# A hybrid decoder layer on one core: a new order of all operations, with more room between TensorE's bursts of small matmuls

## The chip, the core and the metric

The kernel runs on one core of one Trainium2 chip. The core has five engines with their own instruction streams: TensorE (PE, with its weight loads listed apart as PEld), VectorE (DVE), ScalarE (ACT), GpSimd (POOL) and SyncE (SP), which here issues most of the DMA transfers. The metric is the time of one execution on the device in microseconds (us).

## The reference

A decoder sub-layer for 2048 tokens of width 1024, in float32. One input projection gives queries, keys, values and gates of two head groups; the groups run side by side and one output projection joins them:

```python
h = rms_norm(x, norm_w)
proj = jnp.einsum('bsd,de->bse', h, w_in)            # 1024 -> 2816 columns
rq, rk, rv, rg, sq, sk, sv, sg = jnp.split(proj, offsets, axis=-1)
ro = retention(rotary(rq), rotary(rk), rv)           # 4 heads, chunks of 128, a state carried along
ro = group_norm(ro) * ret_norm_w * jax.nn.silu(rg)
so = sliding_window_attention(sq, sk, sv, ...)       # 8 heads, 2 key heads, window 128, sinks, bias
so = so * jax.nn.silu(sg)
x = x + jnp.einsum('bse,ed->bsd', jnp.concatenate([ro, so], -1), w_out)
```

## The kernel before

The four wide products (the input projection in three column groups of 512, 384 and 512 columns, in the program's order, and the output projection) are done by blocks with seven products in place of eight: sums and differences of the blocks of x and of w are formed on VectorE, the seven products run on TensorE, and VectorE and ScalarE add the results together. Each operand is split into a high and a low part (`hi` on ScalarE, `lo` on VectorE), and each product is three passes: high by high, high by low, low by high. In the profile these are the matmuls `acc<-w,x`, with 512, 384 or, at the very end, 128 columns. They run from the first microseconds to the last.

Between runs of `acc` matmuls stand bursts of small ones:

- `m<-ident,kn`: one transpose of normalised keys (16 in all);
- `m<-ks,qT`: the logits of a pair of chunks (8 bursts, 64 matmuls in the program, 128 on the engine, since these take two passes);
- `m<-pT,vn`: weights by values (8 bursts, 72 in the program, 144 on the engine);
- `m<-state,qkT`, `m<-qkT`, `m<-v,qk`, `m<-v,sT`: one step of the retention for a pair of chunks (up to 64 in the program, 128 on the engine). The last step has only the first and the last of the four. Where the fourth part adds to banks that the first part wrote, `outputs` holds its first matmul until the last one of `cross` is through, by an instruction of GpSimd that waits for the one and releases the other (`relay`, `behind`).

Each operation is recorded by `op` with its engine, its reads and writes, and a `go` that issues it. Nothing is issued while it is recorded. `emit` then walks through the table `ORDER` of operation numbers and calls each `go`; where an operation makes a new tile, the next entry of the table `PLACES` says in which numbered buffer it lies, and where it could run on two engines, the table `CHOICE` says on which. `Order.put` ties all instructions into that one order, so each engine gets its instructions in the order of the table. The costs and due times that stand beside the operations aren't read when the kernel is built: they belong to the search that made the tables. Since every instruction is issued from `emit` by way of one helper, nearly all rows of the profile have the same line, L498, and the tiles' names tell them apart.

An entry of `PLACES` decides which earlier tile has to be done with before the new one can be written, and so which waits there are.

Of the kernel before, what the change touches and what calls it, by code (L numbers as in the profile page):

```python
# [124 lines left out]
class Program:  # L125
# [46 lines left out]
    0, 1, 2, 3, 11, 378, 15, 383, 18, 388, 21, 393, 13, 30, 12, 24, 27, 112, 381, 379, 398, 399, 400, 386, 401, 14,  # L172
    380, 402, 403, 404, 405, 406, 407, 382, 408, 409, 4, 16, 17, 384, 410, 387, 385, 411, 412, 33, 389, 390, 115, 413,
    414, 415, 416, 22, 19, 417, 418, 419, 420, 421, 422, 23, 391, 423, 424, 425, 20, 426, 427, 428, 429, 430, 394,
    395, 130, 396, 397, 431, 392, 432, 433, 133, 28, 29, 25, 26, 113, 114, 434, 435, 438, 31, 32, 34, 35, 36, 439,
    116, 436, 440, 118, 121, 117, 119, 120, 131, 38, 132, 40, 42, 122, 64, 41, 43, 123, 75, 437, 442, 136, 443, 441,
    444, 445, 449, 65, 127, 128, 450, 52, 54, 124, 125, 126, 129, 142, 143, 144, 134, 135, 149, 451, 452, 457, 458,
    459, 72, 460, 464, 465, 37, 466, 467, 472, 473, 39, 468, 148, 108, 150, 151, 153, 53, 461, 462, 58, 446, 447, 448,
    158, 44, 463, 45, 139, 140, 141, 474, 475, 55, 476, 137, 138, 477, 478, 46, 213, 145, 469, 159, 60, 479, 480, 481,
    482, 483, 484, 485, 59, 487, 488, 470, 56, 170, 169, 171, 110, 172, 177, 47, 489, 10, 48, 490, 161, 492, 152, 493,  # L180
    160, 491, 494, 109, 173, 162, 164, 155, 214, 495, 500, 501, 299, 305, 179, 146, 57, 191, 180, 147, 486, 502, 503,
    508, 453, 509, 510, 511, 163, 167, 111, 61, 496, 497, 165, 168, 49, 62, 215, 471, 203, 217, 515, 516, 303, 202,
    63, 307, 5, 50, 70, 301, 181, 517, 51, 192, 518, 523, 224, 219, 68, 69, 182, 189, 204, 183, 524, 178, 337, 525,
    526, 527, 528, 529, 530, 531, 311, 533, 534, 535, 536, 185, 190, 300, 504, 538, 507, 205, 209, 206, 225, 71, 309,
    302, 193, 304, 194, 200, 81, 207, 499, 306, 201, 211, 498, 456, 212, 216, 220, 222, 308, 310, 312, 176, 93, 223,
    226, 230, 227, 229, 539, 187, 540, 541, 232, 196, 512, 543, 544, 90, 545, 546, 548, 549, 241, 550, 551, 553, 554,
    555, 233, 234, 84, 556, 558, 559, 333, 228, 239, 240, 542, 331, 9, 235, 236, 560, 561, 563, 197, 184, 313, 237,
    66, 67, 218, 335, 532, 315, 238, 195, 198, 85, 186, 339, 564, 281, 565, 566, 567, 341, 552, 505, 506, 568, 569,
    570, 314, 571, 573, 257, 547, 359, 574, 575, 576, 242, 578, 579, 243, 244, 247, 87, 73, 74, 562, 580, 157, 208,
    581, 321, 86, 78, 245, 246, 94, 248, 557, 332, 334, 249, 250, 513, 537, 336, 338, 340, 454, 95, 258, 343, 357,  # L190
    319, 91, 92, 519, 355, 583, 584, 585, 586, 588, 263, 283, 282, 589, 590, 284, 591, 593, 594, 595, 596, 598, 79,
    80, 599, 600, 601, 251, 252, 349, 317, 253, 345, 264, 7, 210, 347, 603, 604, 605, 577, 514, 520, 521, 254, 606,
    612, 613, 342, 88, 89, 351, 265, 266, 860, 255, 256, 154, 614, 615, 597, 316, 261, 318, 947, 82, 174, 320, 156,
    522, 322, 76, 262, 325, 259, 1412, 344, 346, 348, 350, 572, 616, 617, 582, 621, 622, 623, 624, 352, 361, 175, 6,
    323, 260, 630, 631, 632, 607, 77, 83, 267, 633, 639, 634, 640, 269, 851, 327, 353, 1027, 1028, 938, 625, 641, 270,
    642, 647, 268, 648, 275, 279, 643, 455, 99, 649, 650, 654, 655, 656, 1416, 839, 324, 326, 328, 354, 356, 651, 608,
    609, 657, 661, 658, 329, 277, 231, 358, 635, 102, 1405, 626, 627, 636, 662, 663, 664, 276, 944, 273, 360, 669,
    670, 671, 672, 678, 679, 680, 280, 665, 271, 587, 652, 272, 592, 330, 646, 1417, 673, 681, 687, 688, 188, 278,
    618, 644, 645, 689, 690, 274, 696, 848, 697, 698, 96, 659, 362, 199, 363, 364, 845, 971, 365, 366, 699, 705, 1406,
    367, 368, 941, 369, 370, 371, 372, 660, 706, 707, 1418, 857, 105, 708, 682, 712, 713, 714, 715, 1431, 666, 667,  # L200
    221, 683, 691, 373, 720, 721, 289, 290, 374, 375, 1410, 674, 675, 684, 293, 294, 100, 101, 610, 611, 291, 285,
    292, 376, 377, 602, 700, 722, 723, 728, 939, 729, 950, 940, 97, 98, 637, 676, 619, 620, 653, 106, 107, 692, 694,
    103, 104, 668, 166, 849, 850, 935, 295, 685, 8, 296, 730, 854, 962, 731, 735, 736, 297, 874, 858, 638, 709, 287,
    842, 677, 873, 1473, 298, 737, 738, 286, 744, 745, 739, 740, 742, 695, 743, 840, 859, 686, 746, 747, 701, 288,
    753, 754, 703, 755, 756, 762, 763, 628, 629, 841, 748, 749, 741, 751, 752, 1419, 724, 727, 750, 710, 725, 807,
    757, 1432, 1413, 758, 764, 732, 880, 760, 808, 809, 936, 810, 811, 716, 717, 956, 765, 766, 733, 761, 1414, 951,
    965, 812, 767, 813, 814, 815, 816, 719, 771, 1423, 772, 773, 774, 942, 780, 781, 782, 879, 693, 959, 817, 818,
    819, 820, 702, 711, 718, 775, 776, 778, 726, 861, 734, 821, 822, 1424, 1474, 783, 789, 1434, 759, 768, 1464, 1411,
    1465, 779, 1422, 1427, 790, 791, 843, 937, 1433, 1428, 945, 974, 792, 798, 799, 800, 801, 844, 943, 769, 852,
    1436, 853, 846, 1092, 1437, 1093, 784, 785, 787, 847, 1094, 1095, 866, 1097, 952, 966, 1408, 855, 1098, 1099,  # L210
    1100, 1096, 793, 794, 796, 953, 968, 957, 770, 946, 1404, 1435, 1415, 802, 1102, 856, 1467, 1468, 948, 865, 777,
    1103, 862, 1104, 1105, 788, 949, 885, 1101, 1108, 1109, 1110, 1429, 960, 958, 1440, 1472, 967, 1475, 786, 795,
    1420, 1438, 1111, 1114, 1115, 954, 955, 1425, 1466, 803, 1407, 804, 1116, 704, 864, 875, 876, 1409, 969, 970, 823,
    824, 1469, 963, 964, 1112, 1117, 1458, 1119, 1118, 1120, 1121, 1122, 1124, 1106, 1107, 881, 882, 1477, 1426, 1125,
    1762, 1508, 1430, 1439, 825, 826, 975, 827, 983, 1126, 1127, 961, 972, 1470, 973, 1123, 1441, 1450, 1451, 1421,
    797, 863, 1442, 1443, 1446, 1447, 1130, 1131, 868, 1132, 1133, 1452, 1136, 1137, 1138, 1113, 828, 829, 830, 831,
    832, 833, 1478, 834, 835, 1139, 1140, 836, 837, 867, 980, 977, 1444, 1445, 986, 1141, 1142, 1143, 1144, 1146,
    1147, 1148, 1448, 805, 1454, 886, 1145, 1456, 1149, 1152, 1153, 1154, 838, 1155, 1158, 1159, 1517, 1160, 997,
    1678, 1161, 1471, 1520, 976, 1633, 1516, 869, 870, 981, 887, 888, 978, 1510, 1511, 1449, 989, 1548, 1134, 982,
    1509, 1521, 979, 1156, 1479, 994, 1162, 1157, 1163, 1164, 902, 871, 883, 1549, 872, 1135, 1518, 1512, 1513, 1165,  # L220
    1009, 1166, 1168, 1169, 891, 1455, 1602, 1476, 1170, 1171, 889, 905, 1167, 1174, 1175, 892, 984, 877, 1176, 1177,
    985, 1150, 1151, 1180, 890, 878, 884, 1181, 1182, 1183, 1172, 1173, 1550, 1453, 1457, 911, 1592, 1522, 920, 998,
    999, 1002, 1178, 1557, 1179, 806, 1605, 1606, 1480, 990, 917, 991, 1481, 987, 988, 1459, 1128, 1129, 1185, 895,
    1460, 1184, 1462, 1463, 899, 1593, 995, 996, 1502, 893, 1594, 894, 896, 1186, 1187, 1188, 1189, 1515, 1021, 1005,
    1482, 1483, 1190, 1191, 1192, 1193, 1006, 1519, 1015, 1487, 914, 992, 993, 1195, 1196, 1018, 1493, 1642, 1553,
    1485, 1484, 1197, 1198, 1595, 1488, 1554, 1559, 1012, 1489, 1038, 1003, 1004, 1200, 1201, 1202, 1203, 1199, 1491,
    1205, 1206, 1207, 1000, 1029, 1024, 1208, 1210, 1211, 1212, 1204, 1001, 1551, 1495, 897, 1213, 1215, 1216, 1214,
    1032, 1486, 1494, 1490, 1498, 1041, 1007, 1019, 898, 1492, 1524, 1514, 1497, 1562, 1563, 1686, 1217, 1218, 1496,
    1220, 1221, 1222, 1223, 1597, 1598, 1013, 1014, 1225, 1226, 1227, 1644, 1555, 1219, 1008, 1030, 918, 919, 1601,
# [179 lines left out]
CHOICE = {381: "A", 379: "V", 36: "V", 38: "V", 37: "V", 39: "A", 866: "A", 865: "A", 864: "A", 863: "A", 2189: "A", 2187: "A", 2186: "A", 2188: "A", 2914: "A", 2912: "A", 2915: "A", 2913: "A"}  # L409
# [1461 lines left out]
```

## Time and profile before

| | |
|---|---|
| time, median of 3 runs | 659.26 us (658.93 to 661.24) |
| time of the profiled execution | 658.81 us |
| its span, first to last instruction | 657.04 us |
| PE busy | 652.3 us, 99% of the span |
| DVE busy | 577.4 us, 88% |
| ACT busy | 464.9 us, 71% |
| POOL busy | 41.6 us, 6% |
| granted TensorE clock | 1.00 (2.4 GHz) |
| moved by DMA | 162.94 MB, mean 248 GB/s |

The profiled execution's own time is 1.77 us over its span, and 0.45 us under the median. Times of matmuls in the rows are to be read with care: one that is in flight while the next one starts counts as busy for its whole way through the array, so the mean duration of a matmul is longer than the distance from one start to the next. What a run of matmuls costs is read from the starts of two pieces of the chain, divided by the count.

### The profile page before, as it was taken

Reading aid. Unit: us, or ns where it says so; the run is one execution under the profiler, and the core shown is the slowest. Engines: PE = TensorE matmul, PEld = TensorE weight load, DVE = VectorE, ACT = ScalarE, POOL = GpSimd, SP = SyncE. Lnnn points to the kernel's source line nnn. Section 1 sums busy time; section 2 is a strip of 40 time slices with the busy share of each in tenths; the row PEclk is TensorE's granted clock in tenths of the full one; section 3 lists DMA queues with packets and bytes.
Section 4 is the critical chain, followed back from the end, with each engine's and each line's share of the span. In section 5 each row is a group of like instructions: output and inputs, shape, how many; then the busy total and the mean of one; then the engine's idle time right before and its main releaser. Section 6 shows DMA issues by size and latency. Waiting matters only on the chain.

```text
span 657.0 us, 16143 instructions
## 1 busy us (share of the span) xinstructions
PE 652.3 (99%) x5910; PEld 559.2 (85%) x5910; DVE 577.4 (88%) x1327; ACT 464.9 (71%) x1141; POOL 41.6 (6%) x71
## 2 busy tenths in 40 slices
PE   9999999999999999999999999999999999999998
PEld 7888888888999999998888888888788888888886
DVE  5999986969799998799999999999999999987463
ACT  5755687667898778578997989797999773553200
POOL 0000000010500000000000000000000000323420
PEclk9999999999999999999999999999999999999999
DMA  9978777789989898989999998999989986977986
GB/s 313 345 240 274 226 223 245 250 280 281 266 249 307 237 269 242 270 289 243 303 247 215 288 302 241 272 245 274 295 249 267 231 227 130 169 163 162 140 212 239
DMA packets 156304, 162.94 MB, mean 248 GB/s; under 512 B 62401, under 2 KB 98113, under 8 KB 156225
## 3 DMA queue, kind: packets, MB, share of 16 engines
q1 hardware_dynamic: 151472, 153.52, 79.5%
q0 software_dynamic: 4608, 8.39, 8.3%
q8 instruction: 46, 0.75, 0.5%
q14 instruction: 34, 0.27, 0.1%
q10 hardware_dynamic: 144, 0.00, 0.0%
HBM read 98.63 MB, written 50.66 MB: 227 GB/s over the span
## 4 chain that ended last, share of the span: by engine, by line
PE 97%; DVE 1%; DMA 1%; issue 0%; ACT 0%; SPq 0%
PE acc L498 87%; PE m L498 10%; DMA x<-in_xfirst 1%; DVE r L498 0%; SPq L498 0%; DVE s L498 0%; ACT x L498 0%; DVE sT L498 0%; DVE x L498 0%; DVE w L498 0%; ACT w L498 0%; DVE ro L498 0%; DVE state L498 0%; DVE t L498 0%
## 5 line engine op out<-in xcount | busy, mean ns | idle before, releaser
L498 PE MATMUL acc<-w,x 128*128 128x512 f32 (+1 forms) x2700 | 584.5, 377 | 0.2 <-ACT x L498 0.2
L498 PEld LDWEIGHTS acc<-w,x 128*128 128x128 f32 x2700 | 494.4, 188 | 83.4 <-issue 3.4
L498 DVE TENSOR_TENSOR x<-x 128x512 fp32r<-128x512 f32 (+2 forms) x213 | 139.9, 678 | 7.4 <-ACT x L498 6.0
L498 ACT ACTIVATE x<-x 128x512 fp32r<-128x512 f32 (+1 forms) x180 | 107.8, 620 | 47.8 <-DVE x L498 25.8
L498 DVE TENSOR_TENSOR w<-w 128x512 fp32r<-128x512 f32 (+3 forms) x96 | 61.4, 659 | 4.1 <-ACT w L498 3.9
L498 ACT ACTIVATE lg<-lg,nm 128x160 f32<-128x160 f32 x128 | 53.3, 422 | 5.8 <-DVE nm L498 5.8
L498 ACT ACTIVATE w<-w 128x512 fp32r<-128x512 f32 (+1 forms) x72 | 42.5, 604 | 19.4 <-DVE w L498 9.6
L498 DVE SCALAR_TENSOR_TENSOR w<-w,nw_sb 128x512 fp32r<-128x512 f32 (+3 forms) x72 | 49.9, 704 | 5.9 <-ACT w L498 4.0
L498 DVE TENSOR_TENSOR s<-acc,s 128x512 f32<-128x512 f32 (+1 forms) x64 | 41.4, 654 | 8.8 <-PE acc L498 8.8
L498 DVE CUSTOM_DVE_ANT_0 lg<-m,bias,nsnk 128x160 f32<-128x160 f32 x128 | 41.3, 385 | 1.6 <-PE m L498 1.5
L498 DVE TENSOR_TENSOR t<-acc,t 128x512 f32<-128x512 f32 (+2 forms) x33 | 20.8, 640 | 19.1 <-PE acc L498 19.1
L498 DVE TENSOR_TENSOR r<-acc,t 128x512 f32<-128x512 f32 (+1 forms) x32 | 20.7, 651 | 16.5 <-PE acc L498 15.0
L498 ACT ACTIVATE w<-w,nw_sb 128x512 fp32r<-128x512 f32 (+4 forms) x45 | 29.5, 672 | 4.3 <-DMA w<-in_w_in 2.0
L498 POOL DMA_DIRECT2D c<-in_xtok x8 | 7.2, 943 | 385.4 <-DVE x L498 379.1
L498 ACT ACTIVATE ro<-ro,nmu,rg 128x128 f32<-128x128 f32 x64 | 26.0, 486 | 0.3 <-DVE nmu L498 0.3
L498 DVE STREAM_TRANSPOSE pT<-lg 128x640 f32<-128x640 f32 x32 | 25.8, 831 | 0.0
L498 ACT ACTIVATE x<-go 128x512 fp32r<-128x512 f32 x26 | 15.7, 624 | 13.7 <-DVE go L498 12.1
L498 ACT ACTIVATION_READ_ACCUMULATOR lg<-lg,nm 128x1 f32 x128 | 24.8, 194 | 0.0
L498 ACT ACTIVATE s<-acc 128x512 f32<-128x512 f32 (+1 forms) x32 | 18.1, 565 | 9.3 <-PE acc L498 9.0
L498 DVE TENSOR_TENSOR t<-acc,s 128x512 f32<-128x512 f32 (+1 forms) x32 | 20.7, 655 | 4.1 <-PE acc L498 4.0
L498 ACT ACTIVATE ro<-m 64x256 f32<-64x256 f32 (+1 forms) x48 | 17.8, 379 | 5.7 <-PE m L498 4.0
L498 ACT ACTIVATE c<-acc 128x512 f32<-128x512 f32 (+1 forms) x32 | 17.6, 563 | 4.1 <-PE acc L498 4.1
(141 smaller groups left out, 595.0 us busy)
## 6 DMA issues: line engine op xcount, KB each, us to landing
x<-in_xt SPq DMA_DIRECT2D x76, 256.0 KB, 4.6
planes_dram<-apart SPq DMA_DIRECT2D x48, 256.0 KB, 3.4
x<-s_dram SPq DMA_DIRECT2D x46, 256.0 KB, 4.2
w<-in_w_in SPq DMA_DIRECT2D x40, 256.0 KB, 4.9
xk<-in_xtok SPq DMA_DIRECT2D x32, 256.0 KB, 3.3
s_dram<-x SPq DMA_DIRECT2D x23, 256.0 KB, 3.4
w<-in_w_out SPq DMA_DIRECT2D x20, 256.0 KB, 3.7
vn<-aq_dram SPq DMA_DIRECT2D x8, 576.0 KB, 5.7
```

The costliest lines, as they stand in the source:

```text
L498: return lambda *a, **k: self.order.put(op(*a, **k))
```

## The change

Three tables are replaced; the functions stay as they are. `ORDER` has the same operation numbers in another sequence, `PLACES` has other buffer numbers, and in `CHOICE` operation 37 moves from VectorE to ScalarE (one of four scalings of a tile of weights at the start; the others stay). The tables were searched for again, with a longer time allowed between the moment at which TensorE asks for its next piece of instructions and the moment at which it can run them.

```diff
@@ -169,244 +169,244 @@
 ORDER = (
-    0, 1, 2, 3, 11, 378, 15, 383, 18, 388, 21, 393, 13, 30, 12, 24, 27, 112, 381, 379, 398, 399, 400, 386, 401, 14,
...
-CHOICE = {381: "A", 379: "V", 36: "V", 38: "V", 37: "V", 39: "A", 866: "A", 865: "A", 864: "A", 863: "A", 2189: "A", 2187: "A", 2186: "A", 2188: "A", 2914: "A", 2912: "A", 2915: "A", 2913: "A"}
+CHOICE = {379: "V", 381: "A", 38: "V", 36: "V", 37: "A", 39: "A", 863: "A", 866: "A", 864: "A", 865: "A", 2189: "A", 2186: "A", 2187: "A", 2188: "A", 2913: "A", 2912: "A", 2914: "A", 2915: "A"}
```

The first place is TensorE around the second burst of logits. A row is one form of matmul and how often it follows itself in the program. Before, from the first burst of weights by values to the run that leads up to the second:

```order
L498 MATMUL acc<-w,x 128x384 x30
L498 MATMUL m<-pT,vn 64x128 x32
L498 MATMUL m<-pT,vn 64x256 x8
L498 MATMUL m<-pT,vn 64x128 x32
L498 MATMUL acc<-w,x 128x384 x12
L498 MATMUL m<-ks,qT 32x160 x64
L498 MATMUL acc<-w,x 128x384 x12
L498 MATMUL m<-ident,kn 128x128
L498 MATMUL acc<-w,x 128x384 x84
```

The same place now:

```order
L498 MATMUL acc<-w,x 128x384 x111
L498 MATMUL m<-pT,vn 64x128 x32
L498 MATMUL m<-pT,vn 64x256 x8
L498 MATMUL m<-pT,vn 64x128 x32
L498 MATMUL acc<-w,x 128x384 x21
L498 MATMUL m<-ks,qT 32x160 x64
L498 MATMUL m<-ident,kn 128x128
L498 MATMUL acc<-w,x 128x384 x15
L498 MATMUL m<-ident,kn 128x128
L498 MATMUL acc<-w,x 128x384 x75
```

Between the two bursts stand 21 wide matmuls in place of 12. In the whole program the distance from a burst of weights by values to the next burst of logits was 12, 12, 15, 36 and 12 `acc` matmuls of 384 columns and then 21 of 512; it is now 21, 18, 15, 24 and 15 (of these 6 and 9 around a transpose), and then 12 of 512. The two numbers that follow at the seventh pair have a retention step between. The transposes stood in 13 places of their own and beside a burst in two; now they stand in 11 places of their own and beside a burst in three.

The second place is the densest stretch of TensorE, from the first retention steps to the last burst of logits. Before:

```order
L498 MATMUL m<-v,qk 64x128 x16
L498 MATMUL acc<-w,x 128x512 x12
L498 MATMUL m<-pT,vn 64x128 x32
L498 MATMUL m<-pT,vn 64x256 x8
L498 MATMUL m<-pT,vn 64x128 x32
L498 MATMUL acc<-w,x 128x512 x9
L498 MATMUL m<-state,qkT 64x128 x12
L498 MATMUL m<-qkT 64x64 x16
L498 MATMUL m<-v,qk 64x128 x16
L498 MATMUL m<-v,sT 64x128 x16
L498 MATMUL acc<-w,x 128x512 x15
L498 MATMUL m<-ks,qT 32x160 x64
```

Now:

```order
L498 MATMUL m<-v,qk 64x128 x16
L498 MATMUL acc<-w,x 128x512 x9
L498 MATMUL m<-pT,vn 64x128 x32
L498 MATMUL m<-pT,vn 64x256 x8
L498 MATMUL m<-pT,vn 64x128 x32
L498 MATMUL acc<-w,x 128x512 x12
L498 MATMUL m<-state,qkT 64x128 x12
L498 MATMUL m<-qkT 64x64 x16
L498 MATMUL m<-v,qk 64x128 x16
L498 MATMUL m<-v,sT 64x128 x16
L498 MATMUL acc<-w,x 128x512 x12
L498 MATMUL m<-ks,qT 32x160 x64
```

The wide matmuls between are 9, 12 and 12 where they were 12, 9 and 15, and 21 follow on the logits where 24 did.

The third place is VectorE at the start, with the numbers of the tiles (`x_132` and `x_136` are the second and third block of x to arrive; `x_165`, `x_194`, `x_190` are low parts). Before:

```order
L498 SCALAR_TENSOR_TENSOR w_182<-w_130,nw_sb_70,w_181 128x512
L498 TENSOR_TENSOR x_165<-x_132,x_164 128x256 x2
L498 TENSOR_TENSOR x_194<-x_136,x_193 128x256
L498 SCALAR_TENSOR_TENSOR w_204<-w_138,nw_sb_70,w_203 128x512
L498 SCALAR_TENSOR_TENSOR w_207<-w_134,nw_sb_70,w_206 128x512
```

Now:

```order
L498 SCALAR_TENSOR_TENSOR w_178<-w_130,nw_sb_70,w_177 128x512
L498 TENSOR_TENSOR x_190<-x_136,x_189 128x256
L498 TENSOR_TENSOR x_165<-x_132,x_164 128x256 x2
L498 SCALAR_TENSOR_TENSOR w_207<-w_134,nw_sb_70,w_206 128x512
L498 TENSOR_TENSOR x_190<-x_136,x_189 128x256
```

Half of the third block's low part now stands ahead of the second block's, and the weights of the third block (`w_134`) ahead of those of the fourth (`w_138`). The first 48 `acc` matmuls of TensorE go through the four blocks in the same order as before, and the first eight DMA issues of SP are the same.

## Rows read from the trace of the kernel before

**Rows 1.** The page's busy times: us, share of the span, instructions

```profile
PE 652.3 (99%) x5910; PEld 559.2 (85%) x5910; DVE 577.4 (88%) x1327; ACT 464.9 (71%) x1141; POOL 41.6 (6%) x71
```

**Rows 2.** What PE waited for: us in total, times, longest us

```profile
PE m L498 <- PEq L1859: 0.8, 1, 0.8
PE m L498 <- issue: 0.4, 1, 0.4
PE m L498 <- DVE r L498: 0.2, 1, 0.2
PE acc L498 <- ACT x L498: 0.2, 1, 0.2
```

**Rows 3.** PE by form: count, busy us, mean ns of one, idle before

```profile
L498 PE MATMUL acc<-w,x 128*128 128x512 f32 x2004 | 460.6, 391 | 0.2 <-ACT x L498 0.2
L498 PE MATMUL acc<-w,x 128*128 128x384 f32 x684 | 123.0, 337 | 0.0
```

**Rows 4.** The chain that ended last: start us, us, what

```profile
163.20 8.33 PE acc L498 x48
173.20 2.33 PE m L498 x128
175.54 12.68 PE acc L498 x72
188.33 3.13 PE acc L498 x18
191.56 5.21 PE acc L498 x30
196.77 2.46 PE m L498 x138
...
422.49 3.25 PE m L498 x128
425.74 13.87 PE acc L498 x60
```

**Rows 5.** Timeline of PE around the second burst of logits: start us, us

```profile
196.70 2.53 PE L498 MATMUL m<-pT,vn 32*64 32x128 f32 x144
199.16 2.35 PE L498 MATMUL acc<-w,x 128*128 128x384 f32 x12
201.45 1.41 PE L498 MATMUL m<-ks,qT 64*32 64x160 f32 x65
203.26 1.33 PE L498 MATMUL m<-ks,qT 64*32 64x160 f32 x63 [0.40 <-issue]
```

**Rows 6.** DMA queue that carries PE's instructions: packets, MB, share

```profile
q8 instruction: 46, 0.75, 0.5%
```

**Rows 7.** Timeline of the start, DVE, ACT and PE

```profile
6.97 0.42 ACT L498 ACTIVATE x<-x 128x256 fp32r<-128x256 f32 x1 [2.30 <-DMA x<-in_xfirst]
7.91 0.79 ACT L498 ACTIVATE x<-x 128x256 fp32r<-128x256 f32 x2
8.37 5.97 PE L498 MATMUL acc<-w,x 128*128 128x512 f32 x25 [0.16 <-ACT x L498]
8.71 1.09 DVE L498 TENSOR_TENSOR x<-x 128x256 fp32r<-128x256 f32 x3
```

**Rows 8.** Timeline of PE at the last retention step

```profile
471.04 1.10 PE L498 MATMUL m<-state,qkT 64*64 64x128 f32 x32
472.37 1.10 PE L498 MATMUL m<-v,sT 64*64 64x128 f32 x32 [0.23 <-DVE r L498]
```

**Rows 9.** Timeline of the end, PE, SP and DVE

```profile
647.64 6.28 PE L498 MATMUL acc<-w,x 128*128 128x512 f32 x36
653.25 1.36 SPq L498 DMA_DIRECT2D out<-t  x2
653.95 0.29 DVE L498 TENSOR_TENSOR t<-acc,t 128x128 f32<-128x128 f32 x1 [0.73 <-PE acc L498]
```

**Rows 10.** Busy time by stretch: PE, PEld, DVE, ACT, POOL, PEclk, DMA, GB/s

```profile
300.00:540.00 240.00, 239.77 (x2734) 198.30 (x2718) 234.42 (x601) 211.44 (x511) 0.00 (x0) 1.00 0.95 260
```

**Rows 11.** DVE's forms with the most busy time and the most idle before them

```profile
L498 DVE TENSOR_TENSOR x<-x 128x512 fp32r<-128x512 f32 (+2 forms) x213 | 139.9, 678 | 7.4 <-ACT x L498 6.0
L498 DVE TENSOR_TENSOR t<-acc,t 128x512 f32<-128x512 f32 (+2 forms) x33 | 20.8, 640 | 19.1 <-PE acc L498 19.1
```

465 rows, old and new, of tables (ORDER, PLACES) are left out of this document.

## Prediction

> **What bounds the kernel now.** I read the busy times first. The reader is to see that PE is busy for 652.3 of 657.04 us, so 4.7 us of the span is all that PE is idle by the records [rows 1]. The second view is what PE waited for: four rows, 1.6 us in total, the longest 0.8 us at the very start, and only 0.4 us of data that came late from VectorE and ScalarE [rows 2]. The third is PE by form: the wide matmuls, 2004 of 512 columns and 684 of 384, hold 583.6 of PE's busy 652.3 us [rows 3]. Their true pace is in the chain of waits: 48 in 8.33 us and 30 in 5.21 us are 0.174 us for one of 384 columns, 60 in 13.87 us are 0.231 us for one of 512; a burst of 128 logits takes 2.33 us, or 18.2 ns for one, and a retention step of 128 takes 3.25 us, or 25.4 ns [rows 4]. No count of any form changes, so the time of PE's own work stands, and what the change can move is only the lost time between.
>
> The lost time is small and I name all of it that I can find. At the start, the first run of `acc` stops until 8.37 us for a block of x that landed late [rows 7]. At the last retention step the second part starts 1.33 us after the first, where 32 matmuls need 0.81 us: 0.52 us [rows 8]. After the last wide matmul a last addition and store remain, from 653.95 us to 657.04 us [rows 9]. And one gap lies in the middle of a burst where nothing was waited for: the 65 logits that begin at 201.45 us should have ended 65 x 18.2 ns = 1.18 us later, at 202.63 us, and the next one starts at 203.26 us [rows 5]. That is 0.63 us, of which the table of waits counts 0.4 us, as "issue" [rows 2].
>
> **The change part by part.**
>
> *The gap in the logits.* The queue that carries PE's instructions moved 0.75 MB in 46 packets [rows 6], and PE ran 5910 matmuls and as many weight loads [rows 1]: 16.3 KB and 257 instructions a packet, so one piece is some 128 matmuls. In wide matmuls of 384 columns such a piece lasts 128 x 0.174 = 22 us, in bursts far less. Counted back from the gap, the piece that ended there was 65 logits (1.18 us), 12 wide matmuls (199.16 to 201.45 us, 2.29 us) and 51 of the 144 matmuls of weights by values (2.46 us for 144 [rows 5], so 0.87 us): 4.34 us, and the next one was 0.63 us late. If that is what the gap is, a piece took 5.0 us to come. In the new order 21 wide matmuls stand there: 65 logits, 21 x 0.174 = 3.65 us, and 42 matmuls of 17.1 ns, or 0.72 us: 5.55 us, over 5.0. The amount of work ahead of this place is the same 216 wide matmuls, one burst of each kind and one transpose fewer, so the edge of the piece moves by a few instructions only. The gap goes: -0.63 us. Bounds: nothing (another cause), and -0.63.
>
> The Trainium skill has a rule on this that speaks against the change ("Runtime: NRT & Kernel Launch", the section on instruction fetch): an engine's instructions come in blocks of 16 KiB, 256 of them, through a queue of its own while the block before is running, and crossing a block's edge is mostly hidden. The size agrees with the 16.3 KB worked out above; the gap of 0.63 us without a releaser does not agree with "hidden". By the rule alone the term would be 0 and the sum 0.63 us higher; that result is the first rival below.
>
> *The other close places.* Three pairs stood 12 wide matmuls of 384 columns apart and two of them left no gap in the table of waits, so it also takes an edge at a bad place. Now the closest are two with 15: 15 x 0.174 = 2.61 us and 113 small matmuls at 17.5 ns, 1.98 us, are 4.6 us, 0.4 us under 5.0. The dense stretch has 9, 12 and 12 wide matmuls between its bursts instead of 12, 9 and 15: 3 fewer, 0.7 us less room. Its pieces hold retention steps, where 116 small matmuls at 25.4 ns and 12 wide ones at 0.231 are 5.7 us. The price of these lies between 0 and two gaps of 0.4 us and one of 0.63; I take 0, since a full retention step, 128 matmuls in 3.25 us, left no such gap in seven places before.
>
> *Transposes.* One that stands alone delays the next run by 0.10 us: 188.33 + 3.13 = 191.46, and the next run starts at 191.56 us [rows 4]. Two places fewer: between 0 and -0.2 us, since the transposes themselves stay; I take -0.15.
>
> *Start.* The wait before 8.37 us is for a transfer, by way of ScalarE [rows 7], and the first eight transfers are issued in the same order, so it stays. On VectorE half of the third block now stands ahead of the second. The three pieces that ran at 8.71 us took 1.09 us, 0.36 us each [rows 7]; with one more ahead, the second block's halves are ready by 9.80 us at the latest. PE asks for the first of them eight matmuls after 8.37 us, at 8.37 + 8 x 0.231 = 10.2 us. It is hidden, with 0.4 us to spare; without that cover it would cost 0.36 us.
>
> *One scaling moved from VectorE to ScalarE, new buffers, all the rest of the order.* VectorE loses one of 1327 instructions, and ScalarE, busy 71%, gains one [rows 1]: nothing. For the other engines nearly every row moves. The trace of before bounds this from below: PE lost 0.4 us to late data [rows 2], and no more than that can be won. From above there is no such bound; the mechanism is the slower rival. I take 0, by the nearest rows, since the amounts of work are the same and were hidden but for those 0.4 us.
>
> *Last retention step and end.* The step's second part waits for the first to have gone through PE, passed on by way of GpSimd; in the new order the two still follow each other directly, so its 0.52 us stays. The last product is still cut into 384 and 128 columns with a last addition and store: unchanged.
>
> Sum: 658.81 - 0.63 - 0.15 = 658.03 us for an execution like the profiled one. That one was 0.45 us under the median of the runs shown, so the median comes to **658.5 us**, 0.1% less than before.
>
> **The rivals.**
>
> *The gap was hidden anyway, or only goes elsewhere.* For it: two of the three closest pairs and all retention steps ran through without one. Against it: the gap falls in the middle of a burst whose operands are all there, and no semaphore ended it. Then only the transposes count: 659.26 - 0.15 = 659.1 us.
>
> *Other pieces come late.* For it: two pairs at 4.6 us against 5.0, and a dense stretch with less room. Against it: the shortest distance is longer than before. Two gaps of 0.4 us and one of 0.63 us on top of 658.5: 659.9 us.
>
> *VectorE becomes the bound: slower.* Between 300 and 540 us VectorE is busy for 234.4 of 240 us while PE is busy for 239.8 [rows 10]: 5.6 us is all the idle time it can afford before PE has to wait. VectorE runs its row in order. If the new order puts an addition of a product's result one product too early, VectorE stands for that product, 12 x 0.231 = 2.8 us, and all sums and low parts behind it wait too. Two of these are covered by the 5.6 us; from the third on, PE stops. With four: 11.1 - 5.6 = 5.5 us, 658.5 + 5.5 = 664.0 us. For it: such waits exist, 19.1 us before 33 additions, while the low parts themselves waited only 7.4 us in 213 [rows 11]. Against it: the same amounts fitted before, with 0.2 us of wait on VectorE at PE [rows 2].
>
> **How the numbers follow.** About 0.5%, or 3.3 us, is what a measurement of this kernel can tell from no change. Forecast 658.5 us: chance 0.51. Gap hidden or moved, 659.1 us: 0.26. Other pieces late, 659.9 us: 0.12. All three are within 0.5%: 0.89. VectorE the bound, 664.0 us: 0.08, slower. Faster by more than 3.3 us: if the four waits (1.6 us), what they leave out of the gap (0.23 us) and of the last step (0.3 us), the transposes (0.2 us) and 0.8 us of the first stop all went, it would be 3.1 us; so 0.03, for what I don't see. The range: low end 657.0 us, where the late data and some of the start go too; high end 661.6 us, past the other two cases within 0.5% by the 2 us by which single runs of before differ, and short of the slower rival. It leaves out some 0.15.
>
> **What would show it.** Right: in the new profile PE waits for "issue" less than 0.1 us, the second burst of logits runs 128 in 2.3 to 2.4 us without a break, the last retention step still shows 1.33 us between its parts, PE's idle time in the span falls from 4.7 to about 4.1 us. The first rival: a gap of about 0.6 us without a releaser in another burst. The second: several of 0.4 to 0.7 us. The slower one: PE waits for VectorE or ScalarE for several us between 300 and 540 us, with VectorE's share there no higher than 0.98 and more idle time before its additions. The prediction is wrong if the first stop is no longer at about 8.4 us, if a burst has other matmul counts, or if the median lies outside the range.

## The result, and the profile after

| | before | after |
|---|---|---|
| time, median of 9 runs each | 659.26 us (658.58 to 661.24) | 661.95 us (660.81 to 663.61) |
| ratio | 1 | 1.0039, 95% interval 1.0026 to 1.0051 |
| time of the profiled execution | 658.81 us | 661.48 us |
| its span | 657.04 us | 659.71 us |
| PE busy | 652.3 us | 653.1 us |
| DVE busy | 577.4 us | 575.5 us |

The changed kernel is slower by 0.39%: less than the 0.5% that counted as no change, but with an interval that does not hold 1, and 0.35 us above the predicted range.

The busy times say little: the span grew by 2.67 us, and PE's busy time by 0.8 us. The first view to read is again what PE waited for. In the kernel after (us in total, times, longest us) it is, where [rows 2] had 0.4 us of "issue":

```profile
PE m L498 <- issue: 1.7, 3, 0.8
PE acc L498 <- DVE x L498: 0.7, 1, 0.7
```

Three waits for "issue" where there was one, and a stop for late data that is new. The timeline of PE (start us, us, form, count, idle before) shows where the three are:

```profile
302.08 1.01 PE L498 MATMUL m<-ks,qT 64*32 64x160 f32 x36
303.89 1.85 PE L498 MATMUL m<-ks,qT 64*32 64x160 f32 x92 [0.80 <-issue]
...
369.30 0.83 PE L498 MATMUL m<-v,sT 64*64 64x128 f32 x24
370.67 0.45 PE L498 MATMUL m<-v,sT 64*64 64x128 f32 x8 [0.53 <-issue]
...
399.36 1.05 PE L498 MATMUL m<-v,sT 64*64 64x128 f32 x31
400.72 0.27 PE L498 MATMUL m<-v,sT 64*64 64x128 f32 x1 [0.32 <-issue]
```

All three lie in the middle of a burst, as the gap in [rows 5] did, and nothing released them. The third one stops PE ahead of the very last of 32 matmuls of one kind. Of the burst that had the gap before, the same view now shows 128 in one piece:

```profile
197.02 3.92 PE L498 MATMUL acc<-w,x 128*128 128x384 f32 x21
200.87 2.43 PE L498 MATMUL m<-ks,qT 64*32 64x160 f32 x128
```

So the change did what it was searched for at that place, and lost more at others. The change replaces three tables at once; no run takes them apart.

The stop for data is at the entry of the output projection. PE's timeline there:

```profile
557.69 4.70 PE L498 MATMUL acc<-w,x 128*128 128x512 f32 x20
563.06 5.29 PE L498 MATMUL acc<-w,x 128*128 128x512 f32 x22 [0.67 <-DVE x L498]
568.57 3.67 PE L498 MATMUL acc<-w,x 128*128 128x512 f32 x15 [0.23 <-DVE s L498]
```

VectorE's, ahead of the first of these stops:

```profile
558.48 0.68 DVE L498 TENSOR_TENSOR so<-t,so 128x512 f32<-128x512 f32 x1
561.71 0.69 DVE L498 TENSOR_TENSOR x<-go,so 128x512 f32<-128x512 f32 x1 [2.55 <-PE acc L498]
```

And SP's, where a row is what was issued and how long SP took to issue it:

```profile
549.73 3.86 SPq L498 DMA_TRANSPOSE t<-planes_dram  x2
553.63 2.17 SPq L498 DMA_DIRECT2D go<-turned_dram  x4
```

VectorE stands still for 2.55 us before it can form an operand from `go`, and PE, which needs that operand, stops behind it. The releaser named there, PE, had long been done; the operand `go` comes by the four transfers on SP (a later trace names them), which are issued at 553.63 us, behind two transposes that SP takes 3.86 us to issue. In the kernel before, SP's timeline has the same four behind one:

```profile
548.71 1.23 SPq L498 DMA_TRANSPOSE t<-planes_dram  x1
549.98 2.00 SPq L498 DMA_DIRECT2D go<-turned_dram  x4
```

They were issued 3.65 us earlier there, and PE ran through.

To set the loss against the span I took, in each trace, the distance from every matmul's start to the next, less the usual distance of its form (0.227 us for 512 columns, 0.173 for 384; for the small ones an allowance of 0.040 to 0.120, on the wide side, since they start some 0.02 us apart on average). What is over falls into three heaps: excess over 0.3 us on an edge of TensorE's pieces of instructions (the next section says how these are found), stops of over 0.25 us between 540 and 600 us, and wide matmuls of 512 columns that start 0.43 us apart in place of 0.23 (the lower clock). Each row is one execution. For the two kernels:

| us | span | on edges | late data at the entry | half clock | the rest of the span |
|---|---|---|---|---|---|
| before | 657.04 | 0.62 | 0 | 0 | 656.42 |
| after | 659.71 | 2.28 | 1.22 | 0 | 656.22 |

The 2.67 us between the spans are 1.66 of late pieces, 1.22 of late data, and -0.20 of everything else.

### The profile page after: what moved, and what is told of

Same layout as the page of the kernel before. It is cut to its first block, busy times and chain, and to the rows that moved or that the text cites. A ratio compares the mean times of both kernels' runs of the same rounds, so it can differ in the third digit from the quotient of the medians.

```text
span 659.7 us, 16159 instructions
## 1 busy us (share of the span) xinstructions
PE 653.1 (99%) x5910; PEld 559.0 (85%) x5910; DVE 575.5 (87%) x1326; ACT 464.6 (70%) x1142; POOL 41.7 (6%) x71
## 4 chain that ended last, share of the span: by engine, by line
PE 98%; DVE 1%; issue 1%; POOLq 0%
PE acc L498 87%; PE m L498 11%; DVE x L498 0%; DVE w L498 0%; DVE s L498 0%; DVE go L498 0%; DVE t L498 0%; DVE ro L498 0%; POOLq L498 0%
```

## The experiments

Two theories went in. **Theory A:** TensorE's instructions come in pieces of 256, a gap is a piece that is late, and where in the work the edges between the pieces fall decides how many are late. **Theory D:** the late load at the entry costs what PE's stop there shows. Against A stood that the gaps belong to the work at those places, or that a gap is made good later (called rival B), and for the kernel before that its order stands late pieces better wherever the edges fall (rival C); against D, that something else is late behind the load.

What spoke for A before any experiment: counted in order of start, PE's records (one drain at the start, matmuls, weight loads and waits on semaphores) have each of the four gaps of the two traces ahead of a record whose number, from 0, is 193 past a multiple of 256. The edges can be moved without touching the order: each warm-up matmul at the head of the program is four of PE's instructions, so other warm-up matmuls shift every edge against the work.

### Edges 12 instructions later, and 140 earlier

```diff
-WARM = (256, 256, 256, 256, 128)
+WARM = (512, 512)
```

> The changed kernel with two warm-up matmuls of 512 columns in place of four of 256 and one of 128: 12 instructions fewer at the head of TensorE's queue, the rest of the order untouched, so that every edge between two pieces of 256 instructions falls 12 instructions later in the work. Theory A (most of the loss is pieces of TensorE's instructions that arrive late, and where the edges fall decides it): the gaps at 303.9, 370.7 and 400.7 us (2.27 us together in the changed kernel) shrink to 0 to 0.8 us, the stop at 563 and 568 us stays, time 659.5 to 660.5 us. Rival B (the loss is the late load at 563 us and the other order; gaps in a burst are made good later): the gaps may move, the time stays at 661.5 to 662.3 us.

> The kernel before with the same two warm-up matmuls (12 instructions fewer ahead of the work). Theory A: the gap at 203.26 us (0.62 us) goes or shrinks and no new one over 0.3 us comes; time 658.4 to 659.0 us, ratio 0.9985 to 0.9997. Rival B: 659.3 us, no difference.

The 140 more were forty small warm-up matmuls:

```diff
-WARM = (256, 256, 256, 256, 128)
+WARM = (32,) * 40
-            e.matmul(pw()[:, 0:n], zero.broadcast_to([P, P]), zero.broadcast_to([P, n]), start=True, stop=True)
+            e.matmul(pw()[0:32, 0:n], zero.broadcast_to([P, 32]), zero.broadcast_to([P, n]), start=True, stop=True)
```

> The changed kernel with forty warm-up matmuls of 32 columns (on 32 columns of weights) in place of the five: 140 instructions more ahead of the work, so every edge falls 140 instructions earlier in it. If pieces are late whenever 256 instructions are used up in less than some 5 us (theory A), the edges now fall so that many more pieces lie wholly in dense stretches of narrow matmuls: 5 to 10 us of new gaps, each on an edge of 256; time 666 to 672 us. The start may be later by 0 to 3 us, which the first useful matmul shows. Rival B: only what the start costs, 662 to 665 us.

> The kernel before with the forty warm-up matmuls of 32 columns (140 instructions more ahead of the work). Theory A: 5 to 10 us of gaps on edges of 256 instructions, time 664 to 670 us, so that the kernel before is as exposed as the one after and only the place of its edges made it quicker. Rival C (the order of before is more robust to late pieces, whatever the edges): under 3 us of gaps, 660 to 663 us. The start's own cost is read from the first useful matmul.

Measured, with the kernel before at 659.64 us beside them: the changed kernel with 12 fewer 665.02 us (ratio to before 1.0087, 1.0071 to 1.0103), with 140 more 669.96 us (1.0156, 1.0125 to 1.0187); the kernel before with 12 fewer 659.45 us (1.0000, 0.9987 to 1.0012), with 140 more 669.95 us (1.0164, 1.0145 to 1.0184).

With 140 more both kernels lose 8 to 10 us, as theory A had it; rival B had 662 to 665 us for the changed kernel. The first useful matmul of the changed kernel starts at 4.72 us with them and at 4.77 us without, so the start is not it. PE's timeline of the kernel before with 140 more, around the second burst of logits:

```profile
202.59 0.96 PE L498 MATMUL acc<-w,x 128*128 128x384 f32 x4 [2.05 <-issue]
203.48 2.38 PE L498 MATMUL m<-ks,qT 64*32 64x160 f32 x123
209.54 0.75 PE L498 MATMUL m<-ks,qT 64*32 64x160 f32 x5 [3.67 <-issue]
```

Two stops of 2.05 and 3.67 us that no data explains, where [rows 5] had 0.40: two pieces in a row were used up in the dense stretch. On edges this trace lost 9.49 us, that of the changed kernel 9.62. So with these edges the kernel before is as exposed as the one after, against rival C. With its own edges and with 12 fewer it lost less (0.62 and 1.53 us), so the comparison at 140 is not shown to hold at every place of the edges.

With 12 fewer I was wrong for both kernels. In the changed one I expected the gaps to shrink to at most 0.8 us, and they summed to 2.57. In the kernel before I expected the gap at 203.26 us to go or shrink and 658.4 to 659.0 us; its trace has 1.53 us on edges in place of 0.62, the gap after 71 logits in place of 65, and the time did not change, which by itself is what rival B expected. What did happen is more telling than a gain would have been. The sixth burst of logits, changed kernel with 12 fewer (the view ends at 306 us, inside the burst):

```profile
302.93 1.03 PE L498 MATMUL m<-ks,qT 64*32 64x160 f32 x42
304.93 1.34 PE L498 MATMUL m<-ks,qT 64*32 64x160 f32 x64 [0.98 <-issue]
```

The gap comes after 42 matmuls, where it came after 36: six matmuls with their six weight loads are the 12 instructions. It stays on its edge and moves through the work. That bears out where a gap lies; how long it is, the theory did not foretell.

Most of what this kernel lost beyond the unshifted one is at the entry: its span is 3.0 us longer, of which 1.1 are late data and 1.4 half clock. PE's timeline there:

```profile
564.95 7.34 PE L498 MATMUL acc<-w,x 128*128 128x512 f32 x24 [2.19 <-DVE x L498]
```

And the busy times by stretch (the columns are those of [rows 10]):

```profile
564.90:570.00 5.10, 5.05 (x15) 4.01 (x16) 5.10 (x9) 3.68 (x7) 0.00 (x0) 0.67 0.62 113
570.00:575.00 5.00, 5.00 (x24) 4.14 (x23) 4.73 (x9) 4.89 (x9) 0.00 (x0) 1.00 0.00 0
```

The same operand is late, by 2.19 us, and behind the stop the granted clock is 0.67 of full speed over 5.1 us, a part of it at 1.2 GHz: 15 matmuls where the next five microseconds hold 24. Stop and half clock together are 3.75 us in this trace. In VectorE's timeline of it the same instruction now names the load:

```profile
563.60 0.69 DVE L498 TENSOR_TENSOR x<-go,so 128x512 f32<-128x512 f32 x1 [2.36 <-DMA go<-turned_dram]
```

### A whole piece more, as a control

Against the kernel with 140 more, only the number of small warm-up matmuls differs:

```diff
-WARM = (32,) * 40
+WARM = (32,) * 69
```

> A control to the kernel with 140 instructions more: the changed kernel with sixty-nine warm-up matmuls of 32 columns, 256 instructions more ahead of the work, one whole piece, so that every edge falls on the same instruction of the work as in the changed kernel. The first useful matmul comes some 2 to 3 us later (138 small matmuls at 47 ns), of which the stop for late data at the start may take back a part. Theory A (the place of the edges decides): gaps at the edges of the changed kernel again, near 304 and 401 us above all, 2 to 3.5 us together, and the stop near 563 us; time 661.5 to 665 us. If instead many small warm-up matmuls, or simply more pieces, are what cost 8 us with 140 more: 670 us or over.

663.46 us (ratio to before 1.0061, 1.0044 to 1.0077). The first useful matmul starts at 7.58 us, 2.8 us later, and the rest of the span is 658.66 us, 2.4 us more than the 656.22 of the changed kernel. On edges it lost 2.78 us, at the entry 1.33. More instructions than the 140, and under a third of their loss on edges: it is not the number that costs, but where the edges come to lie. The sixth burst:

```profile
304.17 1.01 PE L498 MATMUL m<-ks,qT 64*32 64x160 f32 x36
305.93 1.85 PE L498 MATMUL m<-ks,qT 64*32 64x160 f32 x92 [0.75 <-issue]
```

36 matmuls and then the gap, on the same instruction as in the unshifted kernel.

### The load moved ahead

```diff
-... 2851, 3211, ... 2886, 2534,
+... 2851, 2534, 3211, ... 2886,
```

Only SP's queue changes: operation 2534, the four transfers `go<-turned_dram`, goes ahead of three of the transposes (the two that it stood behind and one earlier) and of what stands between.

> The changed kernel with one step taken to another place: the load of four tiles go<-turned_dram that SP issues at 553.63 us, behind two DMA transposes, is issued behind the transpose at 538.15 us instead, some 13 us earlier; no other engine's order changes. Theory D (the late load makes TensorE stop at 563.06 and 568.57 us, 0.83 and 0.39 us): VectorE no longer waits 2.55 us for it, both stops go, 1.0 to 1.4 us less than the changed kernel: 660.5 to 661.0 us, ratio to it 0.998. The gaps at 303.9, 370.7 and 400.7 us stay, on the same instructions. Rival: the transposes that are now in front of nothing (t<-planes_dram, 549.73 us, the second of them 2.56 us) are late themselves and stop VectorE at so<-t,so all the same, or the earlier load makes the ones behind it late: 661.5 to 662.3 us.

> The same move in the kernel with two warm-up matmuls of 512 columns (12 instructions fewer ahead of the work), which took 665.02 us. In its trace TensorE stopped for 2.58 us at 564.95 us behind the same load (issued at 554.59 us) and ran at half clock for some 8 matmuls behind it (0.42 us in place of 0.21). Theory D: the stop and the half clock go, 3.5 to 4.5 us less: 660.5 to 661.5 us, with some 2.7 us of gaps on edges of 256 instructions left (at 249.8, 304.9 and 442.5 us). Rival (the stop is only in that one trace, or comes from the gaps ahead of it): 664 to 665 us.

> The same move, with ten warm-up matmuls (eight of 128 columns, two of 64; the columns are 1152 as before) in place of five: 20 instructions more ahead of the work, edges 20 instructions earlier in it. Theory A, that a gap hangs on where the edge lies in a dense stretch: the gaps lie on instructions that are 193 past a multiple of 256 counted with the 20 more, not where they are in the changed kernel; their sum by the distances of the edges in its trace is 0 to 1.5 us in place of 2.27, the time 658.5 to 660.5 us. If a gap hangs on the place in the work (a wait for data or a bank that the trace doesn't name), the three gaps stay at 303.9, 370.7 and 400.7 us: 660.7 us as with the move alone.

Beside the kernel before at 659.33 us: the move alone 661.84 us (ratio 1.0038, 1.0021 to 1.0055), with 12 fewer 659.03 us (1.0005, 0.9989 to 1.0020), with 20 more 661.22 us (1.0027, 1.0014 to 1.0041). With 20 more the gaps lie where theory A puts them, but they sum to 2.88 us, where I expected 0 to 1.5, and the time is over my 658.5 to 660.5 us.

With 12 fewer the move is worth 5 to 6 us (665.02 to 659.03, or 1.0087 to 1.0005 by the ratios, whose intervals lie far apart; the two were measured on different chips): more than the 3.75 us of stop and half clock in the one trace, and 1.5 us better than the best I had expected. The profiled execution of the moved one took 663.69 us, the longest of twelve, so its trace doesn't show how the median came about. Alone the move seemed worth nothing, against my 1.0 to 1.4 us. PE's timeline at the entry with the move alone:

```profile
557.70 13.39 PE L498 MATMUL acc<-w,x 128*128 128x512 f32 x58
571.30 5.02 PE L498 MATMUL acc<-w,x 128*128 128x512 f32 x21 [0.21 <-DVE s L498]
```

The stop at 563 us is gone. But in this execution (664.20 us, the longest of seven) 3.98 us were lost on edges, in place of 2.28, and 1.4 behind one of them at the lower clock: the gain went under in another draw of the gaps, with PE's instructions all the same. So the unmoved kernel was measured again, beside the moved one.

### The changed kernel again, beside the move, and two more shifts

> The changed kernel as it is, beside the three that follow, for a second trace of it. Theory A with fetches of varying delay: gaps again only on instructions 193 past a multiple of 256, 1.5 to 3 us together, but not all at the same edges as in its first trace (303.9, 370.7, 400.7 us); the stop at 563 us is there again (0.5 to 2 us). What is left of the span without gaps, stops and half-clock matmuls is 656.0 to 656.7 us. Time 661.4 to 662.4 us. If the gaps came from the work itself, the same three places with the same lengths.

> The changed kernel with the load go<-turned_dram moved ahead, timed beside the unmoved one on the same chip. Theory D (the late load costs its 1.2 us in most runs): ratio to the unmoved 0.997 to 0.999, 660.3 to 661.2 us. Rival (the stop is hidden by something else late at the same place, a transpose or the gaps ahead of it): the two within 0.4 us of each other. In the trace no stop of TensorE over 0.6 us between 557 and 575 us by theory D.

The other two are the move with `WARM = (512, 512, 128)` and with `WARM = (512,)`.

> The move, with warm-up matmuls of 512, 512 and 128 columns: 8 instructions fewer ahead of the work (edges 8 later). The same with 12 fewer took 659.03 us, with none fewer 661.84 us. Theory A: between them or near the one with 12 fewer, 659.0 to 660.5 us, all loss on edges; what is left of the span without gaps, stops and half clock 656.0 to 656.7 us. If the 2.8 us between those two came from the start (other warm-up, other first clock) the first useful matmul would show it and the time would follow the warm-up's length.

> The move, with one warm-up matmul of 512 columns: 16 instructions fewer ahead of the work (edges 16 later). Theory A: near the one with 12 fewer, 658.5 to 660 us, all loss on edges, the rest of the span 656.0 to 656.7 us; the shorter warm-up may leave the first matmuls at half clock for up to 1 us more, which the start shows.

Beside the kernel before at 659.48 us: the changed kernel 662.16 us (ratio 1.0044, 1.0029 to 1.0059), the move 660.12 us (1.0023, 1.0002 to 1.0043), with 8 fewer 661.96 us (1.0033, 1.0020 to 1.0046), with 16 fewer 660.91 us (1.0026, 1.0015 to 1.0036). The last two are over the ranges that I gave.

Unmoved and moved are 2.0 us apart here and were 0.1 us apart before, when they were not measured side by side, so by time alone the move's worth in the changed kernel stays between nothing and 2 us; its two traces, one with 0.37 us of late data and one with none, are what I go by. The new trace of the changed kernel has gaps at two of the three edges and none at the third. PE's timeline where the piece ends on the last matmul of the burst:

```profile
398.87 1.05 PE L498 MATMUL m<-v,sT 64*64 64x128 f32 x31
401.98 0.27 PE L498 MATMUL m<-v,sT 64*64 64x128 f32 x1 [2.06 <-issue]
402.17 6.20 PE L498 MATMUL acc<-w,x 128*128 128x512 f32 x19
```

And the busy times by stretch around it:

```profile
397.00:401.90 4.90, 2.91 (x123) 2.68 (x116) 4.90 (x12) 3.34 (x9) 0.00 (x0) 1.00 1.33 149
401.90:406.00 4.10, 4.02 (x11) 3.02 (x11) 1.48 (x3) 3.70 (x9) 0.00 (x0) 0.58 0.88 307
```

The same instruction waits 2.06 us that waited 0.32 in the first trace, and here too the clock falls behind it.

With 8 fewer the rival of the move showed. The load is there in time, and VectorE waits for the next thing on SP's queue instead, one of the transposes (its timeline):

```profile
561.85 0.69 DVE L498 TENSOR_TENSOR so<-t,so 128x512 f32<-128x512 f32 x1 [2.64 <-DMA t<-planes_dram]
```

The trace with 12 fewer had it too (3.02 us), that of the move alone for 0.49 us; the other three with the move did not. So the move takes away the first late transfer, and in two traces of six the one behind it made PE stop for 1.8 and 2.1 us. In none of the six does VectorE wait for the load, as theory D has it; in these two its rival, a late transpose, came true.

### All traces together

The sixth burst of logits, matmuls done when the gap comes, by instructions ahead of the work:

| 20 more | none | 256 more | 8 fewer | 12 fewer | 16 fewer |
|---|---|---|---|---|---|
| 26 | 36 (four traces) | 36 | 40 | 42 (two traces) | 44 |

And the span, taken apart as above:

| us | span | on edges | late data at the entry | half clock | rest |
|---|---|---|---|---|---|
| before, 12 fewer | 657.31 | 1.53 | 0 | 0 | 655.78 |
| before, 140 more | 668.88 | 9.49 | 0 | 0 | 659.39 |
| after, again | 662.68 | 3.45 | 1.31 | 1.57 | 656.35 |
| after, 12 fewer | 662.70 | 2.57 | 2.35 | 1.40 | 656.38 |
| after, 140 more | 671.24 | 9.62 | 2.04 | 1.00 | 658.58 |
| after, 256 more | 662.77 | 2.78 | 1.33 | 0 | 658.66 |
| moved | 662.42 | 3.98 | 0.37 | 1.40 | 656.67 |
| moved, again | 658.23 | 2.06 | 0 | 0 | 656.17 |
| moved, 8 fewer | 660.67 | 2.06 | 1.84 | 0 | 656.76 |
| moved, 12 fewer | 661.91 | 1.76 | 2.07 | 1.59 | 656.49 |
| moved, 16 fewer | 660.56 | 2.52 | 0 | 0 | 658.04 |
| moved, 20 more | 659.37 | 2.88 | 0 | 0 | 656.49 |

With the other warm-ups the rest is 655.8 to 656.8 us, whatever the order. With 256 more the start comes later. With 16 fewer the first twelve wide matmuls start some 0.43 us apart, in place of 0.23: the pace that further on goes with the lower clock. With 140 more the rest is 2 to 3 us higher, and the half-clock column, which counts 512 columns alone, misses the reason: in the kernel before with 140 more the granted clock is 0.50 from 208.50 to 215.30 us, from the end of the second stop on, where the wide matmuls have 384 columns.

In all 14 traces PE's records between 12 and 550 us hold 42 pauses of over 0.5 us from one start to the next, and every one of them is at a record 193 past a multiple of 256. Each ends 1.2 to 1.7 us, in the median 1.41 us, after a packet of the queue in [rows 6] has landed.

No kernel here beats the one before by more than its interval; the best, the move with 12 fewer, is equal to it (1.0005). What there is to win is small: 0.62 us on edges is all that the trace of before has in these heaps.

How much work lies in a piece shows how likely it is to come late. Of the pieces of these traces between 12 and 550 us, 16 of the 26 with under 4 us of work ended in such a pause, 21 of the 171 with 4 to 6 us, 5 of the 91 with 6 to 9 us, and none of the 299 with more. The first trace of the changed kernel has 4 pieces with under 5 us of work, that of the kernel before 8: the search made the room that it was asked for, and more pieces came late all the same.

## Why the prediction was wrong

*The gap at the second burst.* Right in the changed kernel, by its own count: 21 wide matmuls made the piece last 5.74 us, the packet landed 2.95 to 4.18 us after the piece began (four traces with the edges unshifted), and with 1.41 us more it was in time. It was not safe, though. In the move with 12 fewer the piece that ends in this burst held 5.79 us of work, its packet landed 4.93 us after it began, and PE paused for 0.62 us. Of the rival that the gap was hidden anyway or only goes elsewhere, the first half falls: a gap that is moved by shifting edges, and of which 140 instructions make 9 us, is the piece's and not the work's. The Trainium skill ("Runtime: NRT & Kernel Launch", the section on instruction fetch) has blocks of 256 instructions, which agrees with the edges found here. "Mostly hidden", as the Trainium skill has it there, holds for most edges: 42 of the 598 edges between 12 and 550 us had a pause of over 0.5 us. The store of 2048 instructions that the Trainium skill gives for TensorE does not show: the piece after the one that runs was not there in these 42 cases.

*The step that failed: "a piece took 5.0 us to come", taken as one number for all edges, and from it "other close places: I take 0".* The term was mis-sized: it measured 2.28 us in the first trace of the changed kernel and 3.45 in the second, for which the prediction had a third case with 1.4 us and a chance of 0.12. The signs of that case came: several waits without a releaser, of 0.80, 0.53 and 0.32 us by the view, and PE waited 1.7 us for "issue" where being right meant under 0.1. The sixth burst of logits shows how. From the edge before to the gap the new order has 5.13 us of work where the old one had 4.54 us at its own edge of the same number, so the longer distance that was asked for is there. But the packet landed 3.41 us after the edge in the old order and 4.84, 4.88, 4.99 and 4.64 us after it in the four traces of the new order with the same edges: with 1.41 us more a piece took 4.8 us to come there, and now 6.1 to 6.4. Nor is it one number for one place: at the edge that ends at 400.72 us it landed 2.27 us after the edge before in one trace, 4.00, 3.77 and 3.12 us in three others, and the gap went from 0.5 to 2.3 us with it. What made the packets land later is not shown.

*"A full retention step left no such gap in seven places before".* True of that trace, but an argument from where the edges lay there: the second and the third gap of the changed kernel are in retention steps, one of them on the last matmul. The sum of 5.7 us for such a piece, "116 small matmuls at 25.4 ns and 12 wide ones", was wrong too. Counted in the trace, the pieces that end at these two gaps hold 6 wide matmuls and none: 4.51 and 3.04 us of work. The pieces of the same numbers in the kernel before hold 14 and 3, 5.88 and 3.71 us, and the second of them was in time by some 0.2 us (its packet landed 2.10 us after the edge).

*Late data: 0.* It measured 1.22 and 1.31 us. I bounded VectorE's row by its idle time, and looked at SP's queue only for its first eight issues. What became late was not an addition in VectorE's row but a load that had come to stand behind two transposes on SP; going through that queue past each move would have shown where it stands, though not what it costs. The rival "VectorE becomes the bound" did not come about: between 300 and 540 us VectorE was busy for 230.9 us, where [rows 10] had 234.4, and PE waited there for pieces alone.

*Transposes, start, last step, end.* The first stop ended at 7.88 us in place of 8.37 [rows 7], which the prediction had named as a sign of being wrong. The 0.5 us can't be put down to the new order: in the second trace of the changed kernel the same matmul starts at 8.43 us, where its first four wide matmuls are followed after 0.39 to 0.57 us each, and in the first trace only the first one is (0.40 us, then 0.23). The last retention step shows 1.25 us between its parts in place of 1.33 [rows 8]. All terms but gaps and late data came to -0.20 us in the first trace, against my -0.15; that the two agree is luck, with 0.5 us of the start in it.

Sum: the term of -0.63 was right for its own gap, and 2.28 us of new gaps and 1.22 us of late data stood at 0. With them 658.5 becomes 662.0 us; 661.95 was measured.

## What to carry to other kernels

Count the instructions of a dense engine, not only its microseconds. Here 37 of the 42 pauses ended pieces of 256 instructions with under 6 us of work; a pause cost 0.5 to 4 us, and every instruction added or dropped earlier in the program moves all later edges. Twelve instructions fewer at the head of the queue brought the changed kernel from 661.95 to 665.02 us, and the one with the load moved from 661.84 (660.12 when measured again) to 659.03 us, with the order untouched. So a difference of 1 to 3 us between two orders says little of the orders until their edges have been shifted too. After a re-ordering, walk through SP's queue as well: in the first trace the load behind two transposes cost 1.22 us, about half of the 2.28 us of the gaps.

## What was not expected of the hardware

- The moment at which the packet of the next piece starts is neither a fixed time nor a fixed number of instructions after an edge: at the two edges looked at above it landed 3.4 to 5.0 and 2.3 to 4.0 us after it, while the packet itself took some 1 us at both. What sets that moment (the sequencer's place, the busy transfer queues) is open; it was not tried.
- Some waits of PE of 1.9 to 2.2 us were followed by a stretch at the lower clock (0.58 of full speed over 4.1 us behind 2.06 us of wait; 0.67 over 5.1 us behind 2.19 us), worth 1.4 to 1.6 us more. Not all were: behind 2.05 us of wait in the kernel before with 140 more the granted clock was 1.00 from 202.50 to 205.50 us, and it fell only in the second stop. Behind 1.19 us of wait, in the move's second trace, the clock stayed at full speed.
- Two DMA transposes on SP took 2.64 us to issue at one place (528.09 us) and 3.86 us at another (549.73 us) in the trace of the changed kernel, so what stands behind them is delayed by more than their count tells.
